# Two-layer trunk on one core: suffix sums and mask of the attention moved to VectorE, GpSimd's products in pieces, a shorter group norm

## The chip, the cores and the metric

The kernel runs on one core of a Trainium2 chip. The metric is device time in microseconds. Five engines work side by side, each through its own queue in program order: TensorE (PE: matrix products, with PEld its weight loads), VectorE (DVE), ScalarE (ACT), GpSimd (POOL), and SyncE (SP), which issues the DMAs. An instruction that waits for another engine holds back all that stand behind it in its own queue.

## The reference

Two layers over 512 tokens of width 2048. The two parts of it that the change touches:

```
# layer 0: stick-breaking attention, 8 heads of 128
z = einsum('bhqd,bhkd->bhqk', qb, kb) * scale
causal = s_idx < t_idx
log_keep = where(causal, log_sigmoid(-z), 0.0)
later = cumsum(log_keep, axis=3, reverse=True) - log_keep
weights = where(causal, exp(log_sigmoid(z) + later), 0.0)
out = einsum('bhqk,bhkd->bhqd', weights, vb)

# layer 1: RWKV-7, 32 heads of 64: a recurrence over the tokens, then a group norm of each head
sa = einsum('bhvk,bhk->bhv', state, -kk_t)
state = state * w_t + sa * (kk_t * a_t) + v_t * k_t
o_t = einsum('bhvk,bhk->bhv', state, r_t)
o = (o - mean) * rsqrt(var + GN_EPS) * gn_w + gn_b
```

`later` is a sum over all later keys: within a block of 128 keys a triangular sum, and over later blocks their whole sums.

## The kernel before

All large products work on operands split into two 32-bit parts, `hi` (rounded, a cast on ScalarE) and `lo` (what is left, a subtraction), made by `split` (L135); `mm3` (L140) then makes three products for one. Weights come in units of 512 or 256 KB by DMA (`wunit`, L146): raw, then `whi` on ScalarE and `wlo` on VectorE, or on GpSimd where `eng` says so.

*Attention* (L261 to L369). `gemm_a` (L158) computes the queries, keys and values of two heads after each other, and after each unit of weights it runs one step of a list of side work (`pump`): so a head's steps stand between the products of the next heads. A head (`head`, L318) lays the transposed scores of a 512 x 512 triangle as 1280 columns: blocks of 128 keys `s` = 0 to 3 with the 512, 384, 256 and 128 queries that may see them. `sp` is the softplus of the scores with the diagonal blocks masked (L340 to L342), `sh` its split. Then, for each block `s` (L347 to L354), TensorE adds up in PSUM: `tri` times block `s`, `ones` times each later block, each for the hi and the lo part, and last `idr` (the identity) times `mbig`, which puts 1e30 where the diagonal block is masked. VectorE subtracts the sums from the scores (`zc`, L357), ScalarE takes the exponential, and after another split the weights meet `v` (L364).

*Scan* (L827 to L1239). The 32 heads go as 16 pairs. For a pair there are: `vproj` (L857), the value projection, 4 units of weights, their `wlo` on GpSimd from the third pair on; `gprod` (L876), Gram products `Z` masked on VectorE; `lanes` (L926), which inverts small triangles: GpSimd lays the diagonals into `nd` (L931), VectorE transposes them (`lt`) and then runs a forward substitution of 15 steps, a product `pr` (L943) and a sum `uc` (L944) each, every one waiting for the one before; `levels` (L962), which builds larger inverses; `vprep` (L906), with the bonus `bv` as a product on GpSimd and a memset of `RS`; `chain` (L1010), the recurrence in 8 steps; and `post` (L1064), the group norm and gate. `slot` (L1148) sets their order: a period has 12 slots, in each of which two pairs' chains go a step under high priority, and then the other work whose due time (tables of L31 and L32) has come. TensorE's order in the scan is as written; the other engines' orders come from a scheduler that gives each ready instruction by priority.

The group norm of a pair (`post`): sum over each head's 64 columns into `gs` (L1072), times 1/64 (L1073), subtract (L1075), square on ScalarE (L1077), sum (L1079), times 1/64 (L1080), then `rsqrt_eps` (L201): square root on ScalarE (L206), `rshgn` = -(v + eps)/2 (L207), reciprocal (L208), one Newton step (L212 to L214), and the product (L1083).

Of the kernel before, what the change touches and what calls it, by code (L numbers as in the profile page):

```python
# [8 lines left out]
F32 = mybir.dt.float32  # L9
F32R = mybir.dt.float32r  # L10
I32 = mybir.dt.int32
AF = mybir.ActivationFunctionType
ALU = mybir.AluOpType
# [4 lines left out]
P = 128  # L18
# [6 lines left out]
GN_EPS = 64e-5  # L25
# [9 lines left out]
class Kernel:  # L35
# [98 lines left out]

    def split(self, hi, lo, src, eng=None):  # L135

        self.nc.scalar.copy(hi, src)  # L137
        (eng or self.nc.vector).tensor_sub(lo, src, hi.bitcast(F32))  # L138

# [6 lines left out]
    def wunit(self, ap, a, b, pool=None, bufs=None, eng=None):  # L146

        pool = pool or self.wp
        ww = self.ww
        raw = self.wp.tile([P, ww], F32, tag="wraw", name="wraw", bufs=3)[:, :a * b].rearrange("p (a b) -> p a b", a=a)  # L150
        self.nc.sync.dma_start(raw, ap)
        kw = {"bufs": bufs} if bufs else {}
        hi = pool.tile([P, ww], F32R, tag="whi", name="whi", **kw)[:, :a * b].rearrange("p (a b) -> p a b", a=a)
        lo = pool.tile([P, ww], F32R, tag="wlo", name="wlo", **kw)[:, :a * b].rearrange("p (a b) -> p a b", a=a)
        self.split(hi, lo, raw, eng)
        return hi, lo
# [43 lines left out]

    def rsqrt_eps(self, pool, v, eps, n, name):  # L201

        nc = self.nc
        T = lambda tag: pool.tile([P, n], F32, tag=tag, name=tag + name, bufs=2)
        sd, hx, t, y = T("rss"), T("rsh"), T("rst"), T("rsy")
        nc.scalar.activation(sd, v, AF.Sqrt, bias=self.eps[eps])  # L206
        nc.vector.tensor_scalar(hx, v, eps, -0.5, ALU.add, ALU.mult)  # L207
        nc.vector.reciprocal(sd, sd)  # L208
        if n == 1:
            nc.vector.tensor_scalar(t, sd, sd, hx, ALU.mult, ALU.mult)  # L210
        else:
            nc.vector.tensor_mul(t, sd, sd)  # L212
            nc.vector.tensor_mul(t, t, hx)
        nc.vector.scalar_tensor_tensor(y, t, 1.5, sd, ALU.add, ALU.mult)  # L214
        return y
# [45 lines left out]
    def attention(self, ctx, W, xs, oh):  # L261
        nc, tc = self.nc, self.tc
        cp = ctx.enter_context(tc.tile_pool(name="attc", bufs=1))
        ap = ctx.enter_context(tc.tile_pool(name="att", bufs=1))
        nc.scalar.preload_act_table_set("natural_log_exp_and_others")

        msk = cp.tile([P, P], F32, name="msk")
# [3 lines left out]
        tri = cp.tile([P, P], F32R, name="tri")  # L271
        ones = cp.tile([P, P], F32R, name="ones")
        mbig = cp.tile([P, P], F32R, name="mbig")
        idr = cp.tile([P, P], F32R, name="idr")
        tmp2 = cp.tile([P, P], F32, name="atmp2")
# [4 lines left out]
        nc.vector.tensor_scalar(mbig, msk, -1.0, -BIG, ALU.add, ALU.mult)  # L280
        nc.vector.tensor_copy(idr, self.ident)
        off = [0, 512, 896, 1152]
        width = [512, 384, 256, 128]
# [7 lines left out]
        for hp in range(4):  # L291
# [11 lines left out]
            def ev_v(n, ps):  # L303
# [5 lines left out]
            self.gemm_a(W, 2048 + hp * 256, xs, ev_v)  # L309
            hs = [self.head(ap, q[n], k[n], vT[n], oh[hp * 2 + n], msk, tri, ones, mbig, idr,  # L310
                            off, width, bank, bcol, boff, bw, TOT) for n in range(2)]
# [5 lines left out]

    def head(self, ap, q, k, vT, o, msk, tri, ones, mbig, idr, off, width, bank, bcol, boff, bw, TOT):  # L318
        nc = self.nc
# [23 lines left out]
        sh = ap.tile([P, 2, TOT], F32R, tag="sh", name="sh")  # L343
        self.split(sh[:, 0, :], sh[:, 1, :], sp)
        yield
        inc = [self.psa.tile([P, S], F32, tag="a", name=f"inc{b}") for b in range(3)]
        for s in range(3, -1, -1):  # L347
            zz = inc[bank[s]][:, bcol[s]:bcol[s] + width[s]]
            for s2 in range(s, 4):
                c0 = (s2 - s) * P  # L350
                lhs = tri if s2 == s else ones
                for j in range(2):
                    mm(zz[:, c0:], lhs, sh[:, j, off[s2]:off[s2] + width[s2]], start=s2 == s and j == 0, stop=False)
            mm(zz[:, :P], idr, mbig, start=False, stop=True)  # L354
        for b in (2, 1, 0):
            sl = slice(boff[b], boff[b] + bw[b])
            nc.vector.tensor_sub(zc[:, sl], zc[:, sl], inc[b][:, :bw[b]])  # L357
        w = ap.tile([P, TOT], F32, tag="e", name="w")
        nc.scalar.activation(w, zc, AF.Exp)
# [467 lines left out]
    def scan(self, ctx, xv, first, mp, ld, ar_d, bk_d, bc_d, g_d, m_d):  # L827
# [78 lines left out]
        def vprep(p):  # L906
# [3 lines left out]
            nc.sync.dma_start(bv, bc_d[p])  # L910
            nc.gpsimd.tensor_mul(bv, s["vT"], bv)

# [151 lines left out]
        def post(p):  # L1064
# [7 lines left out]
            nc.vector.tensor_reduce(sm, O, AX.X, ALU.add)  # L1072
            nc.vector.tensor_scalar(sm, sm, 1.0 / 64, None, ALU.mult)  # L1073
            yield
            nc.vector.tensor_sub(O, O, bc(sm))  # L1075
            sq = tp.tile([P, 8, 64], F32, tag="pt", name="gsq")
            nc.scalar.activation(sq, O, AF.Square)  # L1077
            yield
            nc.vector.tensor_reduce(sm, sq, AX.X, ALU.add)  # L1079
            nc.vector.tensor_scalar(sm, sm, 1.0 / 64, None, ALU.mult)  # L1080
            rs = self.rsqrt_eps(tp, sm, GN_EPS, 8, "gn")
            yield
# [236 lines left out]
```

## Time and profile before

| | before |
|---|---|
| median of 3 runs | 2119.38 us (2112.89 to 2120.28) |
| the profiled execution | 2116.03 us, span 2114.3 us |
| granted clock, mean | 0.99 |
| PE busy, weight loads | 2032.7 us (96%), 1648.2 us (78%) |
| DVE busy | 1295.1 us (61%) |
| ACT busy | 956.5 us (45%) |
| POOL busy | 250.1 us (12%), of it `wlo` of the scan 74.6 us in 56 |
| attention | about 90 to 377 us of the span |
| scan | about 1390 to 1965 us of the span |

The span is from the first to the last instruction of the profiled execution; 1.7 us of its time lie around it. Busy shares are means over stages with different limits; the windows below take them stage by stage. A row of the timeline gives start, duration, engine, line, operation, output and inputs, shape and count, and in brackets the idle time of the engine before it and what ended it. A row of a tile gives the shortest, median and longest duration in ns.

### The profile page before, as it was taken

To read this page: it belongs to the slowest core of one execution; us is meant where nothing else is said; L and a number is where in the kernel's file an instruction comes from. 1 tells how busy PE (TensorE), PEld (TensorE's weight loads), DVE (VectorE), ACT (ScalarE), POOL (GpSimd) and SP (SyncE) were. 2 spreads that over 40 slices of the span, in tenths; PEclk is the share of its full clock that TensorE was granted. 3 is DMA by queue.
4 is the path that set the end of the run, shared out by engine and by line. 5 is a ranking of instruction groups with operands and counts; after the bars stand their busy time and mean duration, and the time that the engine had idled before them with its cause. 6 is when DMAs were issued, how large, how long until landed. Compare 5 with 4: busy or idle time off the path is not lost. (4 is left out here: it accounts for less than half of the span.)

```text
span 2114.3 us, 33769 instructions
## 1 busy us (share of the span) xinstructions
PE 2032.7 (96%) x13139; PEld 1648.2 (78%) x13139; DVE 1295.1 (61%) x2557; ACT 956.5 (45%) x1663; POOL 250.1 (12%) x334
## 2 busy tenths in 40 slices
PE   8999999999999998999999999999999999989996
PEld 7888888888887897777788888877677676666786
DVE  5334344444433358656866776577888988886336
ACT  3345445333221138544654654455555555564211
POOL 0000000000000000233000000013333333310003
PEclk9999999999999999999999999999999999999998
DMA  5222222233333353565365556632232332232733
GB/s 192 91 79 80 80 80 65 85 95 105 100 102 117 111 176 111 157 179 173 110 210 192 197 173 217 202 120 62 91 101 81 96 106 89 85 115 95 235 105 114
DMA packets 214031, 262.97 MB, mean 124 GB/s; under 512 B 15768, under 2 KB 161776, under 8 KB 213104
## 3 DMA queue, kind: packets, MB, share of 16 engines
q1 hardware_dynamic: 213872, 260.83, 38.4%
q8 instruction: 103, 1.69, 0.3%
q14 instruction: 56, 0.46, 0.1%
HBM read 214.32 MB, written 46.47 MB: 123 GB/s over the span
## 5 line engine op out<-in xcount | busy, mean ns | idle before, releaser
L138 DVE TENSOR_TENSOR wlo<-wraw,whi 128x1024 fp32r<-128x1024 f32 (+1 forms) x268 | 313.8, 1175 | 475.9 <-ACT whi L137 464.6
L137 ACT CAST whi<-wraw 128x1024 fp32r<-128x1024 f32 (+1 forms) x324 | 302.9, 938 | 565.3 <-PE ga L143 327.0
L142 PE MATMUL ga<-mx,whi 128*128 128x512 f32 x768 | 299.9, 391 | 3.2 <-ACT mx L137 3.2
L142 PE MATMUL ga<-x,whi 128*128 128x512 f32 x768 | 300.9, 392 | 0.1
L143 PE MATMUL ga<-mx,whi 128*128 128x512 f32 x768 | 300.4, 391 | 0.0
L144 PE MATMUL ga<-mx,wlo 128*128 128x512 f32 x768 | 300.1, 391 | 0.0
L144 PE MATMUL ga<-x,wlo 128*128 128x512 f32 x768 | 299.5, 390 | 0.5 <-DVE wlo L138 0.5
L143 PE MATMUL ga<-x,whi 128*128 128x512 f32 x768 | 299.2, 390 | 0.0
L488 PE MATMUL gb<-whi,mixed 128*128 128x512 f32 (+1 forms) x576 | 198.0, 344 | 3.8 <-DVE s L439 3.8
L490 PE MATMUL gb<-wlo,mixed 128*128 128x512 f32 (+1 forms) x576 | 197.6, 344 | 3.1 <-DVE wlo L138 3.1
L489 PE MATMUL gb<-whi,mixed 128*128 128x512 f32 (+1 forms) x576 | 197.6, 343 | 0.0
L142 PEld LDWEIGHTS ga<-mx,whi 128*128 128x128 f32 x768 | 144.8, 189 | 36.1 <-ACT mx L137 3.6
L143 PEld LDWEIGHTS ga<-mx,whi 128*128 128x128 f32 x768 | 144.7, 188 | 31.5 <-DVE mx L138 0.6
L144 PEld LDWEIGHTS ga<-mx,wlo 128*128 128x128 f32 x768 | 144.8, 188 | 30.6
L144 PEld LDWEIGHTS ga<-x,wlo 128*128 128x128 f32 x768 | 144.2, 188 | 31.2 <-DVE wlo L138 1.0
L142 PEld LDWEIGHTS ga<-x,whi 128*128 128x128 f32 x768 | 144.3, 188 | 29.6 <-ACT whi L137 0.4
L143 PEld LDWEIGHTS ga<-x,whi 128*128 128x128 f32 x768 | 144.3, 188 | 29.1
L488 PEld LDWEIGHTS gb<-whi,mixed 128*128 128x128 f32 x576 | 109.8, 191 | 17.9 <-DVE s L439 5.4
L490 PEld LDWEIGHTS gb<-wlo,mixed 128*128 128x128 f32 x576 | 109.9, 191 | 16.8 <-DVE wlo L138 4.3
L489 PEld LDWEIGHTS gb<-whi,mixed 128*128 128x128 f32 x576 | 109.8, 191 | 12.4
L142 PE MATMUL vps<-mx,whi 128*128 128x512 f32 x256 | 113.8, 445 | 0.0
L138 POOL TENSOR_TENSOR wlo<-wraw,whi 128x512 fp32r<-128x512 f32 x56 | 74.6, 1332 | 257.0 <-ACT whi L137 234.8
(330 smaller groups left out, 3374.8 us busy)
## 6 DMA issues: line engine op xcount, KB each, us to landing
wraw<-in_ev_w_in SPq DMA_DIRECT2D x96, 512.0 KB, 3.6
wraw<-in_ev_w_out SPq DMA_DIRECT2D x32, 512.0 KB, 3.6
wraw<-in_od_w_k SPq DMA_DIRECT2D x32, 512.0 KB, 4.9
wraw<-in_od_w_r SPq DMA_DIRECT2D x32, 512.0 KB, 3.5
wraw<-in_od_w_g SPq DMA_DIRECT2D x32, 512.0 KB, 3.7
wraw<-in_od_w_v SPq DMA_DIRECT2D x64, 256.0 KB, 2.8
ar_d<-pAR SPq DMA_DIRECT2D x16, 512.0 KB, 2.6
bk_d<-pBK SPq DMA_DIRECT2D x16, 512.0 KB, 3.2
```

The source lines that it names most:

```text
L137: self.nc.scalar.copy(hi, src)
L138: (eng or self.nc.vector).tensor_sub(lo, src, hi.bitcast(F32))
L142: mm(ps, ah, bh, start=start, stop=False)
L143: mm(ps, ah, bl, start=False, stop=False)
L144: mm(ps, al, bh, start=False, stop=stop)
L488: mm(ps, ah, bh, start=start, stop=False)
L489: mm(ps, al, bh, start=False, stop=False)
L490: mm(ps, ah, bl, start=False, stop=stop)
```

## The change

In the attention, for queries two or more blocks ahead of a key block, the later key blocks are added up on VectorE ahead of the product: three adds of 128x128 make `rf` (two sums for block 0, one for block 1), `rr` is its split, and one pair of products of `ones` with it stands where there was one pair for each later block. The mask leaves TensorE: `mbig` stays in 32 bits, and four subtractions of 128x128 on VectorE follow the sums. In the scan GpSimd's `wlo` subtraction and the `bv` product are made in four pieces of 128 columns. In the group norm the two scalings by 1/64 go into the instruction behind them, and `rshgn` is a copy with scale and bias on ScalarE.

```
-    def split(self, hi, lo, src, eng=None):
+    def split(self, hi, lo, src, eng=None, parts=1):
         self.nc.scalar.copy(hi, src)
-        (eng or self.nc.vector).tensor_sub(lo, src, hi.bitcast(F32))
+        n = src.shape[1] // parts
+        for q in range(parts):
+            sl = slice(q * n, q * n + n)
+            (eng or self.nc.vector).tensor_sub(lo[:, sl], src[:, sl], hi[:, sl].bitcast(F32))
...
-        self.split(hi, lo, raw, eng)
+        self.split(hi, lo, raw, eng, a if eng else 1)
...
-    def rsqrt_eps(self, pool, v, eps, n, name):
+    def rsqrt_eps(self, pool, v, eps, n, name, scale=1.0):
...
-        nc.scalar.activation(sd, v, AF.Sqrt, bias=self.eps[eps])
-        nc.vector.tensor_scalar(hx, v, eps, -0.5, ALU.add, ALU.mult)
+        nc.scalar.activation(sd, v, AF.Sqrt, bias=self.eps[eps], scale=scale)
+        if n == 1:
+            nc.vector.tensor_scalar(hx, v, eps, -0.5, ALU.add, ALU.mult)
+        else:
+            nc.scalar.activation(hx, v, AF.Copy, bias=-0.5 * eps, scale=-0.5 * scale)
...
-        mbig = cp.tile([P, P], F32R, name="mbig")
-        idr = cp.tile([P, P], F32R, name="idr")
+        mbig = cp.tile([P, P], F32, name="mbig")
...
         self.split(sh[:, 0, :], sh[:, 1, :], sp)
+        rf = ap.tile([P, 384], F32, tag="rf", name="rf")
+        blk = lambda s, t: sp[:, off[s] + (t - s) * P:off[s] + (t - s + 1) * P]
+        nc.vector.tensor_add(rf[:, 256:], blk(2, 3), blk(3, 3))
+        nc.vector.tensor_add(rf[:, 0:P], blk(1, 2), blk(2, 2))
+        nc.vector.tensor_add(rf[:, P:256], blk(1, 3), rf[:, 256:])
+        rr = ap.tile([P, 2, 384], F32R, tag="rr", name="rr")
+        self.split(rr[:, 0, :], rr[:, 1, :], rf)
...
-            for s2 in range(s, 4):
-                c0 = (s2 - s) * P
-                lhs = tri if s2 == s else ones
+            parts = [(tri, sh, off[s], width[s], 0)]
+            if s < 3:
+                parts.append((ones, sh, off[s + 1], P, P))
+            if s < 2:
+                parts.append((ones, rr, 0 if s == 0 else 256, 256 if s == 0 else P, 256))
+            for n, (lhs, t, at, wd, c0) in enumerate(parts):
                 for j in range(2):
-                    mm(zz[:, c0:], lhs, sh[:, j, off[s2]:off[s2] + width[s2]], start=s2 == s and j == 0, stop=False)
-            mm(zz[:, :P], idr, mbig, start=False, stop=True)
+                    mm(zz[:, c0:c0 + wd], lhs, t[:, j, at:at + wd], start=n == 0 and j == 0,
+                       stop=n == len(parts) - 1 and j == 1)
...
+        for s in range(4):
+            nc.vector.tensor_sub(zc[:, off[s]:off[s] + P], zc[:, off[s]:off[s] + P], mbig)
...
-            nc.gpsimd.tensor_mul(bv, s["vT"], bv)
+            for q in range(4):
+                nc.gpsimd.tensor_mul(bv[:, q * P:q * P + P], s["vT"][:, q * P:q * P + P], bv[:, q * P:q * P + P])
...
-            nc.vector.tensor_scalar(sm, sm, 1.0 / 64, None, ALU.mult)
-            yield
-            nc.vector.tensor_sub(O, O, bc(sm))
+            yield
+            nc.vector.scalar_tensor_tensor(O, bc(sm), -1.0 / 64, O, ALU.mult, ALU.add)
...
-            nc.vector.tensor_scalar(sm, sm, 1.0 / 64, None, ALU.mult)
-            rs = self.rsqrt_eps(tp, sm, GN_EPS, 8, "gn")
+            rs = self.rsqrt_eps(tp, sm, GN_EPS, 8, "gn", 1.0 / 64)
```

TensorE's queue in the attention, one head's sums (`inc` is the sum in PSUM, one name for each bank; x2 is the hi and the lo part), before:

```order
L353 MATMUL inc_1418<-sh,tri 128x128 x2
L354 MATMUL inc_1418<-mbig,idr 128x128
L353 MATMUL inc_1418<-sh,tri 128x256 x2
L353 MATMUL inc_1418<-sh,ones 128x128 x2
L354 MATMUL inc_1418<-mbig,idr 128x128
L353 MATMUL inc_1417<-sh,tri 128x384 x2
L353 MATMUL inc_1417<-sh,ones 128x256 x2
L353 MATMUL inc_1417<-sh,ones 128x128 x2
L354 MATMUL inc_1417<-mbig,idr 128x128
L353 MATMUL inc_1416<-sh,tri 128x512 x2
L353 MATMUL inc_1416<-sh,ones 128x384 x2
L353 MATMUL inc_1416<-sh,ones 128x256 x2
```

(two more rows close it, the products of 128 columns and the mask), and in the changed kernel:

```order
L369 MATMUL inc_1433<-sh,tri 128x128 x2
L369 MATMUL inc_1433<-sh,tri 128x256 x2
L369 MATMUL inc_1433<-sh,ones 128x128 x2
L369 MATMUL inc_1432<-sh,tri 128x384 x2
L369 MATMUL inc_1432<-sh,ones 128x128 x2
L369 MATMUL inc_1432<-rr,ones 128x128 x2
L369 MATMUL inc_1431<-sh,tri 128x512 x2
L369 MATMUL inc_1431<-sh,ones 128x128 x2
L369 MATMUL inc_1431<-rr,ones 128x256 x2
```

24 products become 18; where the group stands among the weight products is the same, except in the last head, where a weight product or two change places with it.

GpSimd's queue in one period of the scan (`wlo`: a weight unit's lo part; `bv`: the bonus; `nd`: the diagonals), before:

```order
L138 TENSOR_TENSOR wlo<-wraw,whi 128x512
L911 TENSOR_TENSOR bv<-vT,bv 128x512
L138 TENSOR_TENSOR wlo<-wraw,whi 128x512
L914 MEMSET RS 64x1024
L138 TENSOR_TENSOR wlo<-wraw,whi 128x512 x2
L931 TENSOR_TENSOR nd_10937<-Z_14740,md 32x8x2x16 x2
L931 TENSOR_TENSOR nd_10937<-Z_14741,md 32x8x2x16 x2
```

and in the changed kernel:

```order
L141 TENSOR_TENSOR wlo<-wraw,whi 128x128 x4
L930 TENSOR_TENSOR bv<-vT,bv 128x128 x4
L141 TENSOR_TENSOR wlo<-wraw,whi 128x128 x4
L933 MEMSET RS 64x1024
L141 TENSOR_TENSOR wlo<-wraw,whi 128x128 x8
L950 TENSOR_TENSOR nd_10975<-Z_14889,md 32x8x2x16 x2
L950 TENSOR_TENSOR nd_10975<-Z_14890,md 32x8x2x16 x2
```

The sequence is kept; each product and subtraction is four instructions.

VectorE's queue in the scan, where a pair's group norm stands among the substitution's steps (`gs`: sums, `gsq`: squares, `rssgn`: root and reciprocal), before:

```order
L1079 TENSOR_REDUCE gs<-gsq 128x8
L943 TENSOR_TENSOR pr<-uc,la 128x12x12
L1080 TENSOR_SCALAR gs<-gs 128x8
L944 TENSOR_REDUCE uc<-pr 128x12
L207 TENSOR_SCALAR rshgn<-gs 128x8
L1037 COPY RS<-sa 64x128 x2
L943 TENSOR_TENSOR pr<-uc,la 128x13x13
L208 RECIPROCAL rssgn<-rssgn 128x8
L944 TENSOR_REDUCE uc<-pr 128x13
```

and in the changed kernel:

```order
L1097 TENSOR_REDUCE gs<-gsq 128x8
L963 TENSOR_REDUCE uc<-pr 128x11
L962 TENSOR_TENSOR pr<-uc,la 128x12x12
L214 RECIPROCAL rssgn<-rssgn 128x8
L963 TENSOR_REDUCE uc<-pr 128x12
L218 TENSOR_TENSOR rstgn<-rssgn 128x8
L1056 COPY RS<-sa 64x128 x2
L962 TENSOR_TENSOR pr<-uc,la 128x13x13
L219 TENSOR_TENSOR rstgn<-rstgn,rshgn 128x8
```

Both small instructions between the sum and the reciprocal are gone (as is L1073 ahead of this piece), and the reciprocal (L214) has moved up to two instructions behind the sum. On ScalarE the root and the new copy stand together, ahead of a weight unit's cast instead of behind it. On SyncE one pair of `ml` loads, of 13 in the last part of the scan, moves behind one weight load.

More of the change, by code (lines that the diff above doesn't have):

```diff
@@ L280, in attention @@
         nc.vector.tensor_scalar(mbig, msk, -1.0, -BIG, ALU.add, ALU.mult)
-        nc.vector.tensor_copy(idr, self.ident)
         off = [0, 512, 896, 1152]
@@ L309, in attention @@
             self.gemm_a(W, 2048 + hp * 256, xs, ev_v)
-            hs = [self.head(ap, q[n], k[n], vT[n], oh[hp * 2 + n], msk, tri, ones, mbig, idr,
+            hs = [self.head(ap, q[n], k[n], vT[n], oh[hp * 2 + n], msk, tri, ones, mbig,
                             off, width, bank, bcol, boff, bw, TOT) for n in range(2)]
@@ L316, in attention, with head @@
                 self.side.append(skip if n is None else step(n))
-    def head(self, ap, q, k, vT, o, msk, tri, ones, mbig, idr, off, width, bank, bcol, boff, bw, TOT):
+    def head(self, ap, q, k, vT, o, msk, tri, ones, mbig, off, width, bank, bcol, boff, bw, TOT):
         nc = self.nc
```

## The prediction

> **What bounds the kernel now.** I read the windows first, then the chain that ended last, then single stretches of the timeline. These are the windows' columns and the two stretches that the change touches: the attention (100 to 370 us) and the steady part of the scan (1440 to 1850 us).
>
> ```profile
> core 0: us, PE busy (x) PEld busy (x) DVE busy (x) ACT busy (x) POOL busy (x), PEclk, DMA share, GB/s
> 100.00:370.00 270.00, 269.82 (x1329) 229.10 (x1328) 114.94 (x142) 120.71 (x138) 0.22 (x2) 1.00 0.25 77
> 1440.00:1850.00 410.00, 382.87 (x4750) 284.71 (x4749) 356.28 (x1116) 223.65 (x564) 136.62 (x131) 0.99 0.29 89
> ```
>
> In the attention TensorE never pauses (269.82 of 270) and VectorE is busy for 43%: there a product less is time less, as long as nothing arrives late. In the scan two engines look full, TensorE at 93% and VectorE at 87%. The chain of waits over the same 410 us tells them apart:
>
> ```profile
> by line: DVE pr L943 9.5%; DVE M L1052 7.5%; issue 7.0%; DVE uc L944 6.5%; DVE Z L896 5.7%; DVE RS L1037 5.6%; PE vps L142 4.9%; POOL nd L931 4.3%; PE vps L143 3.7%; PE vps L144 3.5%; DVE xs L1032 3.5%; PE s L1043 2.6%; PE g L890 2.5%; PE x
> ```
>
> The first lines are VectorE's, the forward substitution `pr`, `uc` (L943, L944) in front; TensorE's own come to 17% as far as the row goes. So VectorE's queue sets most of the scan's pace.
>
> The Trainium skill (Perfetto Trace Analysis, Identifying the Most-Contended Engine) says that matmul busy time doesn't tell how near TensorE is to its limit, that LDWEIGHTS time does, and that VectorE's busy share is a fair measure. By that rule the scan is VectorE's (87% against 69% for the weight loads), and the chain agrees; by matmul busy it would be TensorE's, which is my first rival below.
>
> **Attention: the products.** One head's products with `tri`, `ones` and the mask, on TensorE; start, duration, and the time to the next row's start is what a row costs:
>
> ```profile
> 182.71 0.28 PE L354 MATMUL inc<-mbig,idr 128*128 128x128 f32 x1
> 182.82 0.45 PE L353 MATMUL inc<-sh,tri 128*128 128x256 f32 x2
> 183.12 0.34 PE L353 MATMUL inc<-sh,ones 128*128 128x128 f32 x2
> 183.29 0.27 PE L354 MATMUL inc<-mbig,idr 128*128 128x128 f32 x1
> 183.40 0.57 PE L353 MATMUL inc<-sh,tri 128*128 128x384 f32 x2
> 183.80 0.57 PE L353 MATMUL inc<-sh,ones 128*128 128x256 f32 x4
> 184.21 0.27 PE L354 MATMUL inc<-mbig,idr 128*128 128x128 f32 x1
> 184.32 0.67 PE L353 MATMUL inc<-sh,tri 128*128 128x512 f32 x2
> 184.83 0.93 PE L353 MATMUL inc<-sh,ones 128*128 128x384 f32 x6
> 185.59 0.27 PE L354 MATMUL inc<-mbig,idr 128*128 128x128 f32 x1
> 185.70 0.44 PE L142 MATMUL ga<-x,whi 128*128 128x512 f32 x1
> ```
>
> Four mask products go, 0.11 us each: 0.44. The `ones` products of block 1 (two of 256 columns, two of 128) cost 0.41 and become four of 128; two of 128 cost 0.17 (183.12 to 183.29), so 0.34: 0.07 saved. Those of block 0 cost 0.76 and become two of 128 and two of 256, 0.17 + (0.41 - 0.17) = 0.41: 0.35 saved. Together 0.86 us a head, 6.9 for eight.
>
> **Attention: what is put in their place.** A head gets three adds and four mask subtractions of 128x128, a cast of 384 columns on ScalarE and a subtraction of 384 on VectorE. VectorE and ScalarE ahead of the same products, then the last head's subtraction and its first product with it:
>
> ```profile
> 177.74 0.90 DVE L342 TENSOR_TENSOR sp<-sp,msk 128x128 f32<-128x128 f32 x4
> 178.68 1.27 ACT L137 CAST sh<-sp 128x1280 fp32r<-128x1280 f32 x1 [0.56 <-DVE sp L342]
> 179.98 1.49 DVE L138 TENSOR_TENSOR sh<-sp,sh 128x1280 fp32r<-128x1280 f32 x1 [0.20 <-ACT sh L137]
> 364.81 1.49 DVE L138 TENSOR_TENSOR sh<-sp,sh 128x1280 fp32r<-128x1280 f32 x1
> 366.38 0.30 PE L353 MATMUL inc<-sh,tri 128*128 128x128 f32 x1
> ```
>
> Four 128x128 products take 0.90, so 0.22 each. Two adds go ahead of `sh`, which ends at 181.47 and has 0.20 idle before it: 181.7, still ahead of the products, which begin 0.17 before 182.71. The third add (0.22), the cast (1.27 for 1280 columns, so under 0.5) and the subtraction (1.49 for 1280, about 0.5) end near 183.0; the first product with `rr` comes near 183.6. So nothing is late. In the last head `sh` ends at 366.30, 0.08 before its use: three adds make it 0.6 late, once. Behind the products the four mask subtractions (0.88) take back what the earlier end of the products gives to VectorE; that path (exponential, split, last product) has TensorE's other work in front of it, except in the last head, where 0.86 is then lost. **Sum: 6.9 - 0.6 - 0.5 = 5.8, say 6 us**, between 0 (each head's `rr` late) and 7.
>
> **Scan: the shared wait of VectorE and GpSimd.** This is one period of the scan, VectorE and then GpSimd, and two rows of the next period, 30.5 us later:
>
> ```profile
> 1668.66 0.47 DVE L943 TENSOR_TENSOR pr<-uc,la 128x1 f32<-128x1 f32 x1
> 1671.78 0.16 DVE L943 TENSOR_TENSOR pr<-uc,la 128x4 f32<-128x4 f32 x1
> 1676.02 0.86 DVE L943 TENSOR_TENSOR pr<-uc,la 128x81 f32<-128x81 f32 x1
> 1678.93 0.25 DVE L943 TENSOR_TENSOR pr<-uc,la 128x100 f32<-128x100 f32 x1
> 1682.15 1.17 DVE L207 TENSOR_SCALAR rshgn<-gs 128x8 f32<-128x8 f32 x1
> 1667.58 1.53 POOL L138 TENSOR_TENSOR wlo<-wraw,whi 128x512 fp32r<-128x512 f32 x1 [2.36 <-ACT whi L137]
> 1675.51 1.27 POOL L138 TENSOR_TENSOR wlo<-wraw,whi 128x512 fp32r<-128x512 f32 x1 [4.46 <-ACT whi L137]
> 1682.03 1.26 POOL L138 TENSOR_TENSOR wlo<-wraw,whi 128x512 fp32r<-128x512 f32 x1 [4.24 <-ACT whi L137]
> 1706.55 1.26 DVE L943 TENSOR_TENSOR pr<-uc,la 128x81 f32<-128x81 f32 x1
> 1712.74 1.23 DVE L1080 TENSOR_SCALAR gs<-gs 128x8 f32<-128x8 f32 x1
> ```
>
> The 81-element product takes 0.86 or 1.26, the larger 100-element one 0.25. The slow ones end within 0.1 us of the end of a `wlo` subtraction on GpSimd (1675.51 + 1.27 = 1676.78): VectorE's instruction is held until GpSimd's is done. Against an unheld 0.16, 0.25 and 0.16 the period loses 0.3 + 0.6 + 1.0 = 1.9 us, the next 1.0 + 1.1 = 2.1 by these two alone. At about 2.1 a period and 13.4 periods in 410 us, 28 us of VectorE's queue are such waits. What a piece costs, and the instructions that go:
>
> ```profile
> L138 POOL TENSOR_TENSOR wlo<-wraw,whi x56: 1262/1277/1651, 1437.5 to 1864.9; 128x512 fp32r<-128x512 f32 x56
> 1663.70 1.52 POOL L931 TENSOR_TENSOR nd<-Z,md 32x256 f32<-32x256 f32 x2 [0.96 <-DVE Z L896]
> L931 POOL TENSOR_TENSOR nd<-Z,md x64: 718/731/1116, 1409.9 to 1852.5; 32x256 f32<-32x256 f32 x64
> L1080 DVE TENSOR_SCALAR gs<-gs x16: 153/165/1231, 1500.3 to 1947.4; 128x8 f32<-128x8 f32 x16
> L207 DVE TENSOR_SCALAR rshgn<-gs x16: 154/168/1178, 1503.3 to 1947.6; 128x8 f32<-128x8 f32 x16
> L206 ACT ACTIVATE rssgn<-gs,eps x16: 285/301/302, 1500.5 to 1947.6; 128x8 f32<-128x8 f32 x16
> ```
>
> No row shows a GpSimd product of 128 columns. From 512 in 1277 ns and 256 in 731 comes a line of 185 ns plus 2.13 ns an element: 458 ns a piece, an estimate, 1.83 us for four. The bounds are 319 (a quarter of 1277) and 731 (no gain below 256); I take the line. A hold now costs about 0.75 us, 0.6 of the 1.28 that hold it; 0.6 of a piece is 0.27. Holds a period: three in the one, two or more in the next, about 2.7; times 1.43 because GpSimd works longer, less the third that fell on L207 and L1080, so near 3: 0.8 us instead of 2.1, **17 us saved in 13.4 periods**. At 319 ns it would be about 21; at 731 there are 4 to 6 holds of 0.44 and the saving is gone (-4 to +5).
>
> Of the group norm three instructions leave VectorE (L1073, L1080, L207, 0.16 each, starts near 0.12 apart): 0.35 to 0.5 for each of 16 pairs, 6 to 8 us. One copy of some 0.3 (as L206) goes to ScalarE, 55% busy. L1075 stays one instruction of 512. But the reciprocal now stands two short instructions behind the second sum, 0.6 us, in which ScalarE's root (0.30) must be ordered, done and told: a wait of 0 to 0.3, with the copies to `RS` (L1037) queued behind it, which the recurrence's next products on TensorE read. I take 5 net. Ahead of `nd` GpSimd gets 0.55 us more per subtraction; of its two pairs only the second releases VectorE, and GpSimd idles 0.96 before that pair, so nothing; if a subtraction came 1.6 later (731 ns a piece), some 0.5 a period, 6 us. One read of `ml` moves behind a weight load on SyncE: 0 to 2, once; I take 1.
>
> Relief of VectorE: 17 + 5 - 1 = 21 us. Where the chain runs over TensorE or GpSimd it isn't worth its length; I pass on two thirds, **14 us**, with 0 and 24 as bounds.
>
> **Sum.** 6 + 14 = 20 off the profiled execution's 2116.0 gives 2096. That execution lies 3.4 under the median of the runs, 2119.4; going half way to it, I forecast **2098**.
>
> **The rivals.** *TensorE takes over in the scan.* If its 27 us of idle time there are the room, and half of them don't wait for VectorE, the relief ends in other waits: attention's 6 and 0 to 4 more, 2107 to 2112. For it: 93% busy. Against: the chain. Chance 0.16.
>
> *The pieces pass as one.* All four are issued before VectorE's instruction, so it may wait for all. Rows of an earlier stage with both queues full, GpSimd first:
>
> ```profile
> 920.26 3.00 POOL L666 TENSOR_TENSOR xr<-xr,lng 128x512 f32<-128x512 f32 x2
> 923.22 3.46 POOL L667 TENSOR_TENSOR xr<-xr,lnb 128x512 f32<-128x512 f32 x2
> 922.03 1.78 DVE L600 SCALAR_TENSOR_TENSOR mxf<-x,vec,mxf 128x512 f32<-128x512 f32 x1
> 923.73 1.78 DVE L138 TENSOR_TENSOR sqr<-sq,sqr 128x512 fp32r<-128x512 f32 x1
> ```
>
> VectorE finishes one every 1.7 us, GpSimd too: they take turns, one each. Were it otherwise, holds would grow with the square of 1.83/1.28, 28 to 57, two thirds of it left: 38, +10; with the 6 and 5 that is 2116. Chance 0.05. The Trainium skill (SBUF — State Buffer, Who interferes with whom) says that issue order decides and the later one blocks fully; taken to the letter it gives this case, while the rows show turns.
>
> *Each piece holds one (slower).* Turns mean that four pieces can hold four instructions where one held one. If the ladder always has the next two-input instruction ready, a hold is a whole piece: 72 products x 4 x 0.46 = 132 us at most; if half of the pieces do so, 66 against 28, +38, less 11: 2143. It decides when the holds sum to over 0.75 us a product. Against: L944 between two L943 isn't held, nor are the copies from PSUM. Chance 0.06.
>
> *More than the forecast*: waits nearly gone, each passed on whole, 2078 to 2090: 0.11. The forecast, 2090 to 2106: 0.62.
>
> **How the numbers follow.** 0.5% (10.6 us, about what a measurement of this kernel tells from no change) lies at 2109. Faster: 0.62 + 0.11 and a third of the first rival, 0.78; same 0.16; slower 0.06. The range leaves out the third rival and the far ends: 2080 to 2113.
>
> **What will show it.** Right: eight heads' products near 2.3 us instead of 3.2; no L943 above 0.75; a piece near 0.46; a scan period near 30. Wrong: pieces near 0.7, a reciprocal that waits for the root in each period, or a period that stays at 31 with VectorE less busy.

## The result, and the profile after

| | before | after |
|---|---|---|
| median | 2117.52 us (4 runs, 2112.89 to 2120.28) | 2083.39 us (4 runs, 2082.00 to 2084.93) |
| ratio, 95% interval | | 0.9841 [0.982, 0.9862] |
| the profiled execution | 2116.03 us, span 2114.3 | 2082.76 us, span 2081.1 |
| granted clock, mean | 0.99 | 0.992 |
| DVE busy, POOL busy | 1295.1, 250.1 us | 1281.4, 282.9 us |

34 us went, where the forecast's sum had 20. To see where, I compare the start of the same TensorE products in the two traces (before minus after, median over stretches of 20 us): 5.8 us ahead behind the attention (at 400 us), still 5.8 at 620, 10.0 at 1100 and at 1380, 32.1 at 1960, 33.3 at the end. The lead is 0.3 before the attention begins. So the attention gave 5.5, a stage between 620 and 1100 us, which the change does not touch, 4.2, the scan 22.1, and the tail 1.1.

The windows of the changed kernel for the attention and the steady part of the scan, with the columns of the prediction's first fence, and behind them the head of the chain in that part of the scan:

```profile
100.00:370.00 270.00, 269.22 (x1305) 226.81 (x1304) 131.52 (x206) 128.18 (x149) 0.23 (x2) 1.00 0.25 78
1420.00:1830.00 410.00, 394.71 (x5048) 296.13 (x5048) 349.74 (x1138) 233.72 (x599) 174.03 (x344) 1.00 0.31 95
```

```profile
by line: PE vps L145 8.4%; DVE pr L962 7.0%; PE vps L146 6.3%; PE vps L147 5.8%; DVE uc L963 5.5%; issue 4.6%; DVE M L1071 4.1%; DVE RS L1056 4.0%; PE xo L1044 3.9%; PE q L1000 3.7%; PE g L908 3.6%; PE s L1062 3.2%; DVE Z L914 2.9%; DVE xs 
```

In 410 us of scan there are now 5048 matmuls instead of 4750, and VectorE is busy for 349.74 us instead of 356.28 although it does more of the pairs' work. Apart from "issue", the chain's first lines were all VectorE's; now the products of the value projection (`vps`) lead. With the pieces of the chain added up by engine, 1440 to 1850 us of before had 250 us of VectorE and 106 of TensorE; 1430 to 1830 us of after has 160 and 184.

One head of the attention in the changed kernel, VectorE's, ScalarE's and TensorE's rows:

```profile
178.23 1.48 DVE L141 TENSOR_TENSOR sh<-sp,sh 128x1280 fp32r<-128x1280 f32 x1
179.63 0.28 DVE L355 TENSOR_TENSOR rf<-sp,rf 128x128 f32<-128x128 f32 x1
180.50 0.56 DVE L141 TENSOR_TENSOR rr<-rf,rr 128x384 fp32r<-128x384 f32 x1 [0.58 <-ACT rr L137]
...
179.95 0.51 ACT L137 CAST rr<-rf 128x384 fp32r<-128x384 f32 x1 [1.87 <-DVE rf L355]
...
180.68 0.62 PE L369 MATMUL inc<-sh,tri 128*128 128x128 f32 x4
181.14 0.34 PE L369 MATMUL inc<-sh,ones 128*128 128x128 f32 x2
181.31 0.56 PE L369 MATMUL inc<-sh,tri 128*128 128x384 f32 x2
181.72 0.33 PE L369 MATMUL inc<-sh,ones 128*128 128x128 f32 x2
181.88 0.39 PE L369 MATMUL inc<-rr,ones 128*128 128x128 f32 x2
182.11 0.67 PE L369 MATMUL inc<-sh,tri 128*128 128x512 f32 x2
182.62 0.34 PE L369 MATMUL inc<-sh,ones 128*128 128x128 f32 x2
182.79 0.45 PE L369 MATMUL inc<-rr,ones 128*128 128x256 f32 x2
183.08 0.40 PE L145 MATMUL ga<-x,whi 128*128 128x512 f32 x1
```

The products take 183.08 - 180.68 = 2.40 us; before, from 182.54 to 185.70, 3.16. `rr` is done at 181.06, 0.8 ahead of its first use at 181.88, so nothing waits for the sums.

One subtraction in four pieces on GpSimd, and VectorE beside it; then GpSimd's pieces as groups:

```profile
1627.10 1.71 POOL L141 TENSOR_TENSOR wlo<-wraw,whi 128x128 fp32r<-128x128 f32 x4 [3.40 <-DVE RS L1056]
...
1627.20 0.45 DVE L962 TENSOR_TENSOR pr<-uc,la 128x81 f32<-128x81 f32 x1
1627.58 0.40 DVE L1026 TENSOR_TENSOR U<-U,c 32x256 f32<-32x256 f32 x1
1627.91 0.57 DVE L1071 SCALAR_TENSOR_TENSOR M<-s,pcs,m 64x64 f32<-64x64 f32 x2
1628.39 0.41 DVE L1026 TENSOR_TENSOR U<-U,c 32x256 f32<-32x256 f32 x1
1628.84 0.24 DVE L963 TENSOR_REDUCE uc<-pr 128x9 f32<-128x81 f32 x1
```

```profile
L141 POOL TENSOR_TENSOR wlo<-wraw,whi 128x128 fp32r<-128x128 f32 x224 | 100.3, 478 | 222.1 <-ACT whi L137 196.7 <-DVE RS L1056 17.7 <-PE s L1062 4.3
L930 POOL TENSOR_TENSOR bv<-vT,bv 128x128 f32<-128x128 f32 x64 | 27.6, 463 | 33.8 <-DMA bv<-bc_d 26.9 <-issue 6.4 <-DVE U L1013 0.4
```

The 81-element product, 0.86 to 1.26 us before, takes 0.45: it is held to about the end of one piece (0.478 each), and is done 1.16 us before the fourth. `U` and `M`, which come next, read PSUM and are not held, so the other three pieces hold nothing.

The products of the ladder, all sizes together (busy time, mean ns), from 1420 to 1830 us, before and after:

```profile
L943 DVE TENSOR_TENSOR pr<-uc,la 128x121 f32<-128x121 f32 (+14 forms) x204 | 64.9, 318 | 4.9
```

```profile
L962 DVE TENSOR_TENSOR pr<-uc,la 128x1 f32<-128x1 f32 (+14 forms) x215 | 55.3, 257 | 5.6
```

And the group norm's small instructions after:

```profile
L214 DVE RECIPROCAL rssgn<-rssgn 128x8 f32<-128x8 f32 x16 | 3.1, 195 | 0.4 <-ACT rssgn L209 0.4
L209 ACT ACTIVATE rssgn<-gs,eps 128x8 f32<-128x8 f32 x16 | 4.8, 302 | 7.4 <-DVE gs L1097 7.4
L213 ACT ACTIVATE rshgn<-gs 128x8 f32<-128x8 f32 x16 | 3.1, 194 | 0.0
```

The reciprocal waits for the root for 0.4 us in all 16 pairs together.

### The profile page after: what moved, and what is told of

It is laid out like the page before. It is cut to its first block, busy times and chain, and to the rows that moved or that the text cites. A ratio compares the mean times of both kernels' runs of the same rounds, so it can differ in the third digit from the quotient of the medians.

```text
span 2081.1 us, 33937 instructions
## 1 busy us (share of the span) xinstructions
PE 2015.5 (97%) x13091; PEld 1635.0 (79%) x13091; DVE 1281.4 (62%) x2572; ACT 960.2 (46%) x1687; POOL 282.9 (14%) x550
## 5 line engine op out<-in xcount | busy, mean ns | idle before, releaser
L141 POOL TENSOR_TENSOR wlo<-wraw,whi 128x128 fp32r<-128x128 f32 x224 | 100.3, 478 | 222.1 <-ACT whi L137 196.7
```

The lines of the kernel that those rows point to most:

```text
L141: (eng or self.nc.vector).tensor_sub(lo[:, sl], src[:, sl], hi[:, sl].bitcast(F32))
```

## The experiments

My theory after the result: the scan's gain is the held time of VectorE, given back one for one. Rivals: two thirds are given back and something else adds to it; or the pieces help by another order of things on GpSimd. For each run I add up the held time in the scan (1400 to 1950 us): VectorE's instructions are grouped by line and shape, the duration at the lower third of a group counts as unheld, and what an instruction takes beyond it, if over 0.08 us, counts as held. The gain in the scan is the growth of the lead over the trace of before from 1380 to 1960 us. The column of the clock adds up (1 - granted clock) over the scan of each trace: full clock that TensorE lost there. A second trace of before (e11) shows how far that can move a gain: it lost 3.4 us more of clock in the scan and took 4.0 us longer for it.

| kernel | held, us | gain in the scan, us (traces) | clock lost in the scan, us | ratio to before, 95% interval |
|---|---|---|---|---|
| before | 27.1 | | 8.5 | |
| e6: 2 pieces (769 ns each) | 14.2 | 11.5 | 6.8 | 0.992 [0.9906, 0.9933] |
| e2: 4 pieces (480 ns) | 6.4 | 19.1 | 6.8 | 0.99 [0.9884, 0.9916] |
| e7: 8 pieces (334 ns) | 9.2 (11.5) | 11.2 | 10.2 | 0.9921 [0.9907, 0.9934] |
| e5: memset instead (524 ns) | 6.7 | 23.5 | 5.1 | 0.9869 [0.9855, 0.9882] |
| e3: group norm alone | 20.0 | 6.8 | 8.5 | 0.9947 [0.9931, 0.9964] |
| e4: 4 pieces and group norm | 5.2 | 21.9 | 5.1 | 0.9882 [0.9864, 0.99] |
| after | 4.9 | 22.1 | 6.8 | 0.9841 [0.982, 0.9862] |

With eight pieces the rule misleads, as some groups are held in more than two thirds of their rows. Against the unheld durations of the other kernels, and with overlapping rows counted once, e7's held time is 11.5 us; the other rows change by 0.3 at most.

### The parts of the change, each alone

**e1, the attention's part** (`attention` and `head` as in the changed kernel, all else as before):

```diff
-            mm(zz[:, :P], idr, mbig, start=False, stop=True)
+        self.split(rr[:, 0, :], rr[:, 1, :], rf)
...
+        for s in range(4):
+            nc.vector.tensor_sub(zc[:, off[s]:off[s] + P], zc[:, off[s]:off[s] + P], mbig)
```

> Only the attention's part of the change. Both theories: 5.8 us less than before (ratio near 0.997), all of it gained by 380 us of the span, 0.8 a head for the first seven heads; the scan keeps its 575 us and its period of 31 us. If the 4 us that the changed kernel gained between 740 and 1060 us belong to the attention's part, they show here again; if they are scatter between executions, they don't.

2104.47 us (2103.71 to 2108.74), ratio 0.9948 [0.9932, 0.9964]: 12 us by the medians, twice the forecast. By the traces the lead is 5.5 at 400 us, as forecast, and 10.8 at 1100: the other half arises in a stage whose instructions are the same in both kernels (see e8, e11 and e12).

**e2, GpSimd's pieces** (`split` with `parts`, and the loop over `bv`):

```diff
-        self.split(hi, lo, raw, eng)
+        self.split(hi, lo, raw, eng, a if eng else 1)
```

> Only GpSimd's pieces; every other engine's order is that of before. Theory of the holds: VectorE's holds fall from 27 us to 7 to 10, the scan is 14 to 17 us shorter, about 2101 (ratio 0.992 to 0.994). Rival, the order: the gain came from the group norm's shorter queue and the new place of its instructions, and the pieces alone give 0 to 5 us.

2095.20 us (2093.94 to 2097.77), 21.5 us less than before's 2116.72 in the same comparison. This edit alters no instruction on any other engine, and it alone gives more than the 14 us that I gave the whole scan. Held time falls by 20.7 us, the gain in the scan is 19.1.

**e3, the group norm** (`rsqrt_eps` and `post` as changed):

```diff
-            nc.vector.tensor_scalar(sm, sm, 1.0 / 64, None, ALU.mult)
-            rs = self.rsqrt_eps(tp, sm, GN_EPS, 8, "gn")
+            rs = self.rsqrt_eps(tp, sm, GN_EPS, 8, "gn", 1.0 / 64)
...
+            nc.scalar.activation(hx, v, AF.Copy, bias=-0.5 * eps, scale=-0.5 * scale)
```

> Only the group norm's part; GpSimd keeps whole subtractions. Theory of the holds: 5 us for the three instructions, and of the 9 us that L207 and L1080 were held half moves to other instructions: 6 to 10 us less, holds near 20 us. Rival, the order: 12 us less or more.

2106.55 us (2102.10 to 2108.08), 10 us less. Its held time falls from 27.1 to 20.0 us, and it gains 6.8 in the scan. The reason is that two of the instructions that leave, L207 and L1080, were themselves held: nine of these rows lasted 0.6 to 1.1 us longer than unheld, 8.9 us together. Part of that moved to the ladder: its products are held for 19.2 us in e3, 17.0 in before.

**e4, both scan edits** (the diffs of e2 and e3 together).

> Pieces and group norm together, attention as before: the changed kernel without its attention part. Theory of the holds: the sum of both parts alone, about 20 to 24 us less (ratio 0.989 to 0.9905). If the parts need each other, it is clearly more than their sum; if they take the same holds away, less.

2092.11 us (2089.06 to 2093.26), 24.6 less, where 21.5 and 10.2 would add up to 31.7. Held time falls to 5.2: the two edits take the same waits away, and neither can take them twice.

### The size of a piece, and no reads at all

**e5**: GpSimd writes zeros to `wlo` without reading; the low part of these weights is left out.

```diff
-        (eng or self.nc.vector).tensor_sub(lo, src, hi.bitcast(F32))
+        if eng:
+            eng.memset(lo.bitcast(F32), 0.0)
+        else:
+            self.nc.vector.tensor_sub(lo, src, hi.bitcast(F32))
```

> The kernel before, with the scan's subtractions on GpSimd replaced by a memset of wlo to zero (the low part of W is left out of these products). GpSimd then reads nothing for them. Theory (VectorE's two-input instruction is held until GpSimd's two-input one is done, and each microsecond held is passed on whole): the holds of VectorE in the scan fall from 27 us to under 3, a period from 31 to about 29.2 us, and 23 to 28 us go: 2089 to 2094. Rival (only two thirds are passed on, as the prediction took): 15 to 18 us. Rival (GpSimd's length, not its reads, is what VectorE waits for; the pieces helped by letting something else through): holds stay above 10 us and under 12 us go.

2088.60 us (2087.14 to 2090.77), 28.1 less than 2116.73. The amount is the theory's (23.5 us in the scan, of which 3.4 can be the clock, and 4.2 ahead of it); the held time is not as low as it expected: 6.7 us are left, 3.0 of them in `pr` beside the `bv` product, which still reads, and 3.2 in `rshgn`, ten times about 0.3 us beside the memset. So a memset of 0.524 us holds a small instruction too.

**e6, e7**: as e2, with two pieces of 256 or eight of 64 columns for `wlo` and `bv`, in e6:

```diff
-        self.split(hi, lo, raw, eng)
+        self.split(hi, lo, raw, eng, 2 if eng else 1)
```

> The kernel before, with wlo and bv on GpSimd in two pieces of 256 columns instead of one of 512. From 1277 ns for 512 columns and 478 for 128 a piece of 256 is 744 ns. Theory (a hold lasts to the end of the piece that runs; about as many instructions are held as before): holds of 27 us fall by 744/1277 to about 15, and 10 to 14 us go, half of what four pieces gave: 2103 to 2107. Rival (each piece holds an instruction of its own): holds stay at 22 us or more and less than 6 us go. Rival (the size of a piece does not matter, the gain of four is one of the order on GpSimd): 19 to 22 us go.

2098.60 us (2097.29 to 2103.89). Held time falls to 14.2 us, as expected from the piece's length, and the traces give 11.5 in the scan. The medians give more, 18, which is outside the 10 to 14 that I expected; the profiled execution was the slowest of the five. The rival by which each piece holds an instruction of its own (22 us held) falls. The one by which a piece's size does not matter (19 to 22 us) falls by the held time and the traces; by the medians it would be almost met.

> The kernel before, with wlo and bv on GpSimd in eight pieces of 64 columns. From 1277 and 478 a piece of 64 is 345 ns, a subtraction 2.8 us against 1.9 in four. Theory (a hold lasts to the end of the running piece): the 6.4 us of holds that four pieces left fall to about 4, worth 2 us, and GpSimd's additional 0.85 us per subtraction lies in its idle time: 20 to 25 us go, 2092 to 2097. Rival (GpSimd becomes late for nd, which releases VectorE's transpose): less than 17 us go, with VectorE waiting for nd.

2099.51 us (2099.28 to 2105.47): 17 us, at the edge of the rival's bound, and less than four pieces gave. Held time rises instead of falling. Of the 11.5 us, 5.6 are `pr`, as much as with four pieces: the product of 9 elements now falls on a piece of GpSimd's in 12 of 16 pairs and takes twice as long. Another 5.4 are the scaling of `gs` beside the memset of `RS`. The product of 9 elements with four pieces, then with eight (busy time, mean ns):

```profile
L947 DVE TENSOR_TENSOR pr<-uc,la 128x9 f32<-128x9 f32 x14 | 2.4, 173 | 0.5
L949 DVE TENSOR_TENSOR pr<-uc,la 128x9 f32<-128x9 f32 x14 | 4.3, 310 | 0.5
```

The wait of the transpose `lt` for `nd` on GpSimd is 26.5 us in 14 pairs, against 24.9 with four pieces, which is small. The rest of the difference in the traces is the clock, most of it in the first periods, here of eight pieces, then of four:

```profile
1440.00:1480.00 40.00, 38.17 (x432) 28.54 (x431) 27.13 (x84) 19.18 (x48) 16.39 (x52) 0.91 0.16 48
1480.00:1520.00 40.00, 36.69 (x436) 27.50 (x436) 29.04 (x94) 20.38 (x51) 18.81 (x51) 0.91 0.19 60
```

```profile
1440.00:1480.00 40.00, 38.39 (x469) 29.11 (x470) 27.75 (x86) 19.61 (x49) 15.29 (x33) 0.96 0.18 54
1480.00:1520.00 40.00, 37.13 (x497) 27.93 (x494) 32.58 (x111) 21.61 (x54) 16.65 (x33) 1.00 0.27 86
```

The granted clock is 0.91 over 80 us, 7 us of TensorE's full speed, against 0.96 and 1.00 (1.6 us); over the whole scan it is 10.2 us against 6.8. GpSimd's subtractions take 134.1 us in all instead of 100.8. Why four beats eight by 4 us in the medians, where the clock of single executions differs, is not settled beyond that.

### The five microseconds outside both parts

**e8**: the sums of the attention's part without its mask, so the products with `idr` and `mbig` stay; of e1's diff it has only the second line and what makes `rf`.

> The kernel before with one half of the attention part: the sums over later blocks go ahead of the products with ones, while the mask stays a product. By the prediction's rows the products get 0.42 us a head shorter, 3.4 in eight, less 0.6 in the last head: about 3 us by the end of the attention. If the further 5 us that the whole attention part gained between 600 and 1080 us belong to the sums, about 8 us go in all (2109); if they belong to the mask, 3 (2114). If they depend on the time at which the later stages begin rather than on either edit, something in between, and the gain lies again between 640 and 1060 us.

2109.89 us (2107.25 to 2112.63), ratio 0.9968 [0.9957, 0.998]. The lead is 2.9 us at 400, as forecast, and 8.2 at 1100. So half of the edit brings the whole additional 5 us; and e5, which changes nothing ahead of the scan, has 4.2 there too. The additional gain isn't a saving of the attention's own products.

**e11, e12**: the kernel before, and e1, once more.

> The kernel before once more, unchanged, for a second trace of it. If the 4 to 5 us between 600 and 1080 us, which the attention part, the sums alone and the kernel without holds had and the pieces and the group norm had not, are a matter of the single execution, this trace may differ from the first by some microseconds in just that stretch, and by under 1 us in the attention and the scan. If they belong to the kernel, it agrees with the first to within 1 us there too.

> The attention part alone once more, unchanged, for a second trace of it. By the single execution: a gain of 5.5 us by 400 us again, and between 600 and 1080 us anything from 0 to 5. By the kernel: 5.5 and then 4 to 6 again.

The second trace of before (2117.87 us) differs from the first by under 0.3 us up to 740 us, is 2.1 ahead at 800 and 2.5 at 1100, and loses 3.9 around 1440. The second trace of e1 (2112.53 us, against 2103.71) has the same 5.5 at 400 us and is level with the first at 980 (0.5), then loses 4.3 by 1070 and 2.4 more at 1440. So a large part of it varies with the single execution. The windows show what differs (the third figure from the end is the granted clock); before, first trace:

```profile
750.00:760.00 10.00, 9.10 (x63) 9.10 (x64) 7.12 (x10) 2.94 (x3) 0.00 (x0) 0.83 0.43 133
800.00:810.00 10.00, 5.00 (x37) 4.39 (x35) 7.95 (x22) 8.29 (x23) 1.50 (x6) 0.80 0.32 132
810.00:820.00 10.00, 8.96 (x28) 6.87 (x29) 9.70 (x16) 9.41 (x17) 2.25 (x3) 0.68 0.42 120
```

e1, first trace:

```profile
750.00:760.00 10.00, 10.00 (x85) 10.00 (x85) 4.51 (x5) 4.20 (x4) 0.00 (x0) 1.00 0.76 233
800.00:810.00 10.00, 6.92 (x21) 5.29 (x22) 8.13 (x13) 8.11 (x16) 2.73 (x6) 0.66 0.42 122
810.00:820.00 10.00, 9.98 (x45) 7.94 (x44) 10.00 (x16) 9.05 (x15) 0.00 (x0) 1.00 0.21 68
```

e1, second trace, where it falls behind:

```profile
1050.00:1060.00 10.00, 10.00 (x38) 8.06 (x38) 7.65 (x11) 5.00 (x8) 0.31 (x2) 0.83 0.59 195
1440.00:1450.00 10.00, 10.00 (x88) 8.00 (x89) 5.09 (x14) 2.78 (x9) 2.92 (x4) 0.67 0.01 2
```

Between 600 and 1080 us before lost (0.17 + 0.20 + 0.32) x 10 = 6.9 us of full clock, e1 3.4: 3.5 of the 5 us. The other difference is in TensorE's pauses at `gb` around 660, 705 and 750 us, where VectorE's `s` waits for a read of the residual: 3.8 us in before, 1.2 in e1. Together that is 6.1 us, more than the 5.3 that e1 gained here, so not all of it was passed on. The row of these waits (us in total, times, longest) in before and in the changed kernel, 600 to 780 us:

```profile
PE gb L488 <- DVE s L439: 3.8, 3, 2.0
PE gb L506 <- DVE s L457: 1.1, 3, 0.5
```

These pauses are not scatter alone: they come to 0.6 to 1.5 us in all six traces with the attention's part or its sums, and to 3.3 to 4.0 in seven of the eight without (e5: 1.0). So some 2.5 us go with the attention's part, although no instruction of that stage differs; why the wait is shorter there is not shown. The clock's loss in that stage doesn't go with it: 3.4 to 6.8 us with the part, 1.7 to 6.8 without. The medians also have an additional gain, 6.7 us in e1 and 4 in e8 beyond what the attention itself gave. Whether a kernel that pauses less keeps its clock up more often is left open; the mean granted clocks of whole executions point that way (before 0.985 to 0.992, 0.989 on average, in the 30 runs beside the experiments; after 0.991 to 0.992 in 4).

### What bounds the changed kernel

**e10**: the changed kernel without one VectorE multiplication of 0.68 us a pair.

```diff
-            nc.vector.scalar_tensor_tensor(m, m, 0.5, gt, ALU.mult, ALU.mult)
```

> The changed kernel without the last multiplication of the group norm on VectorE (the product of gm with 0.5 and the gate ldg is left out): 0.68 us less of VectorE's queue in each of 16 pairs, 11 us. Theory (TensorE now ends most of the waits of the scan, as the kernel without holds shows it): 0 to 4 us less than the changed kernel, 2079 to 2083. Rival (VectorE is still the bound and its time is worth nearly its length): 8 to 11 us, 2072 to 2076.

2082.50 us (2080.11 to 2085.66), 0.9849 [0.9835, 0.9863] of before, where the changed kernel has 0.9841: 16 instructions of 0.685 us, 11 us, taken out of VectorE's queue are worth nothing now. VectorE's busy time fell by 5.4 us only, from 1281.4 to 1276.0.

**e9**: the changed kernel with one of the four `nd` products on VectorE.

```diff
-                nc.gpsimd.tensor_mul(nd2[r, :, :16]...
+                (nc.vector if q == 3 else nc.gpsimd).tensor_mul(nd2[r, :, :16]...
```

> The changed kernel with the fourth of the four nd products (L950) on VectorE instead of GpSimd. In the changed kernel VectorE stands idle for about 1.64 us a pair until GpSimd's second pair of nd (1.52 us) is done; with the last on VectorE (some 0.4 us of work in that idle time) the wait ends after one, 0.7 us earlier, 11 us in 16 pairs. Theory (time of VectorE's queue in the scan is still worth nearly its length): 8 to 11 us less than the changed kernel, 2072 to 2076. Rival (TensorE sets the pace now): 0 to 4 us less. Rival (VectorE's product is held by GpSimd's third one, or comes ahead of other work): no gain, 2083 or a little over.

2075.80 us (2074.84 to 2077.24), 0.9818 [0.9805, 0.9832] of before: the fastest of all, 7.6 us under the changed kernel's median (taken on another chip; before is 2114.67 here and 2117.52 there). By the ratios the gain is 5 us, and their intervals overlap; but e10, run beside e9 and no faster than the changed kernel, is 6.7 us slower without overlap. By the traces 8.0 us are gained, all behind 1380; 3.4 of them can be the clock, of which e9 lost 3.4 us in the scan and the changed kernel 6.8. VectorE's transpose and its wait for `nd`, after and in e9:

```profile
L955 DVE STREAM_TRANSPOSE lt<-nd 128x512 f32<-128x512 f32 x15 | 10.7, 711 | 25.1 <-POOL nd L950 25.1
```

```profile
L955 DVE STREAM_TRANSPOSE lt<-nd 128x512 f32<-128x512 f32 x14 | 10.0, 712 | 8.6 <-POOL nd L950 8.6
L950 DVE TENSOR_TENSOR nd<-Z,md 32x256 f32<-32x256 f32 x14 | 8.9, 637 | 0.5
```

The wait falls from 1.67 to 0.61 us a pair, for 0.64 us of work on VectorE, so `lt` starts some 0.4 us earlier; 16 pairs make 7 if all of it is passed on. The chain in the same part of the scan, in e10 and in e9:

```profile
by line: PE vps L145 11.3%; PE vps L146 8.6%; PE vps L147 7.6%; PE g L908 6.7%; PE xo L1044 5.2%; issue 4.7%; DVE pr L962 4.5%; PE s L1062 4.0%; DVE uc L963 3.6%; DVE M L1071 3.5%; DVE RS L1056 3.1%; POOL nd L950 3.1%; PE q L1000 2.9%; DVE 
```

```profile
by line: PE vps L145 14.5%; PE vps L146 10.9%; PE vps L147 10.7%; PE g L908 7.3%; PE xo L1044 6.9%; PE s L1062 5.6%; PE q L1000 5.3%; PE sa L1055 3.9%; PE bt L920 3.6%; PE xo L1047 3.1%; PE xo L1076 2.9%; PE c L1010 2.7%; DVE pr L962 2.4%; 
```

In e10 `nd` on GpSimd (3.1%) and the ladder behind it are still on the chain; in e9 `nd` is no longer among the lines shown and TensorE's lead throughout (332 of 400 us, with the pieces added up). What the scan waited for in the changed kernel was not the length of VectorE's queue but, at least in part, the way from the Gram product over `nd` to the ladder. So the theory that TensorE ends most waits held for work taken off VectorE's queue (e10), and fell where that wait itself was shortened (e9).

## Why the prediction was right, and where it was too small

*The attention* (6 us): right in size and place. A head's products went from 3.16 to 2.40 us, 0.76 instead of 0.86. In e12 the lead grows by 0.8 us with each of the first seven heads and falls by 0.1 with the last, for which the terms were 0.86 less 1.1. In all traces with the whole part the attention gave 5.5.

*The scan* (14 us) is the term that was mis-sized; it measured 22.1, of which 1.7 can be the clock. Three steps of it:

- *What the holds come to.* "28 us of VectorE's queue are such waits" measured 24.7 in those 410 us, and 27.1 in the whole scan. "17 us saved" measured 21.1 and 22.2. A piece's price was right (458 forecast, 478 and 463 measured), but fewer instructions are held than the three a period that I took: 17 in 13.4 periods, for 0.21 us on average. Behind the held product of 81 elements stand `U` and `M`, which are not held.
- *The group norm's instructions, "5 net".* Alone they gained 6.8 us with 7.1 of held time gone (e3), and on top of the pieces 2.8 with 1.2 (e4 against e2). What is left for the instructions themselves is 0 to 2 us. So the relief as a whole, 21 us forecast, came out at 22 to 24 by two errors that offset each other, which is luck.
- *"I pass on two thirds."* This was the largest error. The share was that of VectorE in the whole chain, and the right question was whether the held instructions lie on it. Two stretches of the chain of before (start, length, what) answer it:

```profile
1706.55 0.30 DVE pr L943
1706.85 0.88 issue
1707.73 0.40 DVE U L1007
...
1712.61 0.21 DVE pr L943
1712.83 1.15 DVE gs L1080
1713.97 0.21 DVE uc L944
```

The held `pr` stands there as 0.30 of `pr` and 0.88 of "issue", the held `gs` as 1.15. Added up over the scan, 25.1 of the 27.1 us of held time lie on the chain. As the traces stand, 22.2 us saved are 22.1 gained, and e2, e3, e4 and e6 lie within 1.6 us of one for one too (e5 gained 3 more than it freed, e7 4 less). With the difference of the clock to before taken off, the gains are 76 to 99% of the held time freed, 92% in the changed kernel. So more than two thirds was passed on in every run, and one for one is not shown. "Issue" fell from 7.0% of the chain to 4.6%.

*The middle of the program* was in no term: 4.2 us, of the granted clock of one execution against another, and of the shorter pauses at `gb`. Before's profiled execution lost 3.4 us more of clock there than after's; a prediction from one trace has that error.

*The rivals.* TensorE takes over: not within this change's gain. Just behind it relief of VectorE's queue stops paying (e10), but there it is the wait for `nd`, not TensorE alone, that sets the pace (e9). The pieces pass as one: shown wrong by the 0.45 us at 1627.20. The rule of the Trainium skill (SBUF — State Buffer, Who interferes with whom) is that whoever issues first gets the shared pair of ports for the whole instruction, and the other fully blocks. The trace agrees for the one piece that runs (the product ends 0.1 us behind it), and not for the reading that I gave the rule, by which all pieces issued ahead go first. Each piece holds one: wrong, the held time of `pr` fell from 17.0 us with whole products to 12.0 with two pieces and 5.5 with four, and did not grow with eight. More than the forecast, "waits nearly gone, each passed on whole, 2078 to 2090", given 0.11, is what came in time: the waits nearly went, and most of what they cost was passed on. The 2090 to 2106 that had 0.62 was missed.

*The signs named.* Products near 2.3: 2.40. No L943 above 0.75: the longest is 0.60. A piece near 0.46: 0.478 and 0.463. A period near 30: 28.9 and 29.8 by turns. The reciprocal's wait: 0.4 us in all. The Trainium skill's reading of the contended engine (Perfetto Trace Analysis, Identifying the Most-Contended Engine), VectorE at 87% against 69% for the weight loads, agreed with what the relief was worth. In the changed kernel it gives 85% against 72%, still VectorE, and there e10 speaks against it.

## What to carry to other kernels

When a stall is to be removed, ask of the stalled instructions themselves whether they lie on the chain, "issue" behind them included; an engine's mean share of the chain says little about it. Where one engine's instruction holds another's, the hold lasts about until what is running ends, so shorter pieces on the engine that has time to spare help, until their own cost tells. When relief of an engine stops paying, look for an engine's idle time that ends with one and the same small producer in every period: there an instruction may pay on the busier engine.

## What was not expected of the hardware

- TensorE's granted clock falls to 0.5 for single stretches of 3.4, 6.8 or 10.2 us, at other places in each execution of the same kernel (0.50 in each window of 1 us from 752 to 754 in the first trace of before). Each costs 1.7, 3.4 or 5.1 us of full clock. In the 14 traces 71 of 72 such stretches ahead of the program's end begin within 6 us behind a pause of TensorE of at least 0.5 us, or at its very end; of all moments from 600 to 1080 and from 1400 to 1960 us 17% lie so. This is a large part of the scatter: before ran from 2111.09 us at a mean clock of 0.991 to 2122.93 at 0.986.
- A memset on GpSimd (0.524 us for 512 columns) held VectorE's 128x8 `rshgn` for some 0.3 us, ten times in e5; each time `rshgn` ended within 0.03 us behind the memset.
- A GpSimd product of two 32-bit operands took 334, 478, 769 and 1277 ns for 64, 128, 256 and 512 columns of 128 partitions: about 0.2 us are fixed.
